# Summing a conditioning vector over 128 partitions: one-column matmuls, or whole-tile transposes and a VectorE row sum

## The chip, the cores and the metric

The kernel runs on one core of a Trainium2 chip. The metric is device time in microseconds (us) of one execution. Before the change the median of three runs is 3439.34 us (3439.0 to 3443.46). All intervals below come from one profiled execution of the kernel before, whose own time stands in the table.

## What is computed

Two transformer blocks with two layers each, on 512 tokens of 1024 features, in fp32; the second block also carries 256 context tokens. Every layer's norms and residuals are steered by six conditioning vectors of 1024 numbers, and it is these vectors that the change touches. Cut to that, the reference is:

```python
cond = jax.nn.silu(c)                                   # 1024 numbers
for layer in range(2):                                  # first block
    mod = (cond @ ada_w[layer] + ada_b[layer])[:, None, :]      # (1024) x (1024 x 6144)
    shift_m, scale_m, gate_m, shift_f, scale_f, gate_f = jnp.split(mod, 6, axis=-1)
    ...
    x = x + gate_f * swiglu(h, ffn_w_in[layer], ffn_w_out[layer])
sc, scc = jax.nn.silu(c), jax.nn.silu(c_ctx)
for l in range(2):                                      # second block
    mx = sc @ w_ada[l] + b_ada[l]                       # for the tokens
    mc = scc @ w_ada[l] + b_ada[l]                      # for the context, same weights
    ...
```

## The kernel before

Feature-major layout: a tensor of 1024 features lies as 8 tiles of 128 partitions by tokens. Every large product is made of three fp32r matmuls (lines 243 to 245): activations and weights are split into a high and a low part (`hh`, `hl`, `gh`, `gl`; `whi`, `wlo`), and high x high, low x high and high x low are added up in PSUM. Weights come by DMA as `raw` tiles of 128x1024 (two buffers), ScalarE casts them to `whi` (line 172) and VectorE makes `wlo` (line 173), three buffers each. One such unit feeds 24 matmuls.

`ffn` (lines 486 to 515, inside `dense`) is the feed-forward stage: for every 128 hidden features TensorE makes a gate and an up product (24 matmuls each), ScalarE takes the silu into `t2a` (line 505), VectorE multiplies (line 507, `t2b`) and the result is split into `gh` and `gl`; after each group of hidden features `out_proj` multiplies by the third weight and VectorE adds into `x` (line 528). Six PSUM banks (`dn`, `d`) rotate through these products, and two more (`tp`) serve small things: the norms' statistics, broadcasts of a column, and the sums that the change is about.

The conditioning vectors are background work. `ada_tasks` (line 288) cuts the product of `cond` and a 1024 x 6144 matrix into groups of 512 output columns, and each group into 8 tasks, one per 128 rows of the matrix. A task loads a 128x512 tile `araw` (line 299) and VectorE multiplies it by a per-partition scalar and adds it into `acc`, 128x512 (lines 308 and 310). After the eighth task `acc` holds 128 partial sums of each of 512 columns, one in every partition, and they must be added over the partitions and turned so that the 512 numbers stand as 128 partitions x 4 columns of `mod`. Four matmuls do that (line 319): each takes 128 columns of `acc` as the stationary operand and a column of ones as the moving one, and writes one column of a `tp` bank. VectorE adds the bias while it copies the four columns out (line 322).

`tick` runs up to three tasks between matmul blocks of a stage, so the group's matmuls stand in TensorE's queue between two blocks of 24. Tile's scheduler sets the order of the instructions on each engine from the program's order and its own estimates. Where `conds` has two vectors, one loaded tile serves two accumulators, and the two groups' sums follow each other.

The vectors of the first block's first layer are made in the opening and in the attention stage. The others are made in three `ffn` stages: those of the first block's second layer (12 groups, one vector), of the second block's first layer (12 groups, two vectors) and of its second layer (4 groups with two vectors, 8 with one). After the first 32 tasks of the middle one `hnorm_now` makes the context's first norm: squares and their column sums (lines 369, 370), a small transpose (375), a power on GpSimd (352), a broadcast by transposes (359).

Of the kernel before, what the change touches and what calls it, by code (L numbers as in the profile page):

```python
# [14 lines left out]
ALU = mybir.AluOpType  # L15
AX = mybir.AxisListType

P = 128
# [121 lines left out]
class Net:  # L140
# [144 lines left out]
        return self.pa.tile([P, 512], F32, tag=tag, bufs=2, name=tag)  # L285


    def ada_tasks(self, w, groups, conds, dsts, bias, bufs=3, bank="st", on_pe=()):

        nc = self.nc
        tasks = []
        for n, g in enumerate([2 * g + i for g in groups for i in range(2)]):
            st = {}
            for k in range(KD):
                def step(g=g, k=k, st=st, pe=n in on_pe):
                    raw = self.accp.tile([P, 512], F32, tag="araw", bufs=bufs, name="araw")
                    nc.sync.dma_start(raw, w[k * P:(k + 1) * P, g * 512:(g + 1) * 512])
                    for i, cond in enumerate(conds):  # L300
                        s = cond[:, k:k + 1]
                        if pe:
                            if k == 0:
                                st[i] = self.psum(bank)
                            nc.tensor.matmul(st[i][:1], lhsT=s, rhs=raw, start=k == 0, stop=k == KD - 1)
                        elif k == 0:
                            st[i] = self.accp.tile([P, 512], F32, tag=f"acc{i}", bufs=1, name="acc")
                            nc.vector.tensor_scalar(st[i], raw, s, None, op0=ALU.mult)
                        else:
                            nc.vector.scalar_tensor_tensor(st[i], raw, s, st[i], op0=ALU.mult, op1=ALU.add)  # L310
                    if k == KD - 1:
                        for i, dst in enumerate(dsts):
                            acc, rows = st[i], 1 if pe else P
                            if pe:
                                acc = self.accp.tile([1, 512], F32, tag="row", bufs=1, name="row")
                                nc.scalar.copy(acc, st[i][:1])
                            ps = self.psum(bank)
                            for j in range(4):
                                nc.tensor.matmul(ps[:, j:j + 1], lhsT=acc[:, j * P:(j + 1) * P], rhs=self.one[:rows],
                                                 start=True, stop=True)  # L320
                            s = slice(g * 4, g * 4 + 4)
                            nc.vector.tensor_add(dst[:, s], ps[:, :4], bias[:, s])
                tasks.append(step)
        return tasks
# [1484 lines left out]
    def block1(self, x):  # L1809
        nc, a, fx = self.nc, self.a, self.fx  # L1810
        cond = self.cond

        def gain(g, i, mod, grp):
            return self.gain(self.v(g, i, 8), mod, grp)

        mod = fx.tile([P, 48], F32, tag="modx", bufs=2, name="mod")
        b = self.v("ada_b", 0, 48)
        with self.pool("rope", side="right") as rp:
            with self.dense():
                for k in range(0, KD, 4):  # L1820
                    nc.sync.dma_start(x[:, k:k + 4], a["xT"][k * P:(k + 4) * P].rearrange("(k p) t -> p k t", p=P))
                self.c_inv = self.load_const(rp, "inv")
                self.c_sgn = self.load_const(rp, "sgn")
                with self.pool("acc", side="right") as self.accp:
                    rope = self.rope_tables(rp, self.accp)
                    self.causal = self.load_const(rp, "causal", BF16)
                    self.lt01 = self.load_const(rp, "lt01")
                    self.ltneg = self.load_const(rp, "ltneg", BF16)
                    self.negtri = self.load_const(rp, "negtri", F32R)
                    self.work["u"] = (self.accp, 8, "t2u", T)  # L1830
                    tasks = self.ada_tasks(a["ada_w"][0], (1, 0), [cond], [mod], b, 12, "dn", (1, 3))
                    A = fx.tile([P, KD], F32, tag="A1", bufs=3, name="A")
                    h, ((stats, apply),) = self.hnorm(x, T, A, mod[:, 0:8], size=T)
                    w = a["attn_w_in"][0][:, 1024:1280]
                    loads = self.load_ahead(*[(w, 0, k, "k") for k in (0, 4)])
                    for i in range(32):
                        tasks[i // 16 * 16 + (1 - i % 2) * 8 + i % 16 // 2]()
                        if i == 7:
                            stats()
                        if i == 15:  # L1840
                            self.gain_scale(A, self.v("norm_mix_g", 0, 8), mod, 1)
                    for load in loads:
                        load()
                    apply()
                self.rope_cs = rope()
            self.bg += self.ada_tasks(a["ada_w"][0], (2, 3, 4, 5), [cond], [mod], b, 2)
            out = []

            def norms(g, i, grp, *loads):
                h, steps = self.hnorm(x, T, gain(g, i, self.mod, grp + 1), self.mod[:, grp * 8:grp * 8 + 8])  # L1850
                out.append(h)
                self.loads = self.load_ahead(*loads)
                return steps

            self.mod = mod
            self.attention(x, h, mod[:, 16:24], a["attn_w_in"][0], a["attn_w_out"][0],
                           lambda: norms("norm_ffn_g", 0, 3, *self.ffn_first(*self.gate_up(a["ffn_w_in"][0]))))
        with self.dense():
            g_in, gate = a["gdn_w_in"][0], mod[:, 40:48]
            mod = self.mod = fx.tile([P, 48], F32, tag="modx", bufs=2, name="mod")  # L1860
            self.bg += self.ada_tasks(a["ada_w"][1], (1, 0, 2, 3, 4, 5), [cond], [mod], self.v("ada_b", 48, 48))
            self.ffn(*self.gate_up(a["ffn_w_in"][0]), a["ffn_w_out"][0], [(out[0], x, T, gate)],
                     lambda: norms("norm_mix_g", 8, 0, (g_in[:, 4096:4112], 0),
                                   *[(g_in[:, c:c + P], 0) for c in (D, 0)]))
        with self.psum_pool(**GDN_BANKS) as self.pp:
            self.gdn(x, out[1], mod[:, 16:24], a["gdn_w_in"][0], a["gdn_w_out"][0],
                     lambda: norms("norm_ffn_g", 8, 3, *self.ffn_first(*self.gate_up(a["ffn_w_in"][1]))))
        return out[2]
# [58 lines left out]
```

## Time and profile before

| | us |
|---|---|
| median of 3 runs (lowest, highest) | 3439.34 (3439.0, 3443.46) |
| the profiled execution | 3443.76 |
| its span, first to last instruction | 3442.0 |
| TensorE (PE) busy, share of the span | 3273.7, 95% |
| VectorE (DVE) busy | 2202.9, 64% |
| ScalarE (ACT) busy | 1274.1, 37% |
| mean granted TensorE clock | 0.981 |

PE is TensorE's matmuls, PEld its weight loads, which overlap them. An instruction's duration in a timeline is longer than the distance to the next one, because matmuls are pipelined: what one costs in a row of matmuls is read from start to start. "Idle before" an instruction is time in which its engine had nothing to run, and the name behind the arrow is what ended it.

### The profile page before, as it was taken

What the parts mean: (1) busy time and instruction counts of PE and PEld (TensorE: products, weight loads), DVE (VectorE), ACT (ScalarE), POOL (GpSimd) and SP (SyncE); (2) the same over time, 40 slices, a digit from 0 to 9 for tenths busy, and PEclk for the clock granted to TensorE, in tenths of its full rate; (3) what the DMA queues carried; (4) which work ended last, traced back from release to release, by engine and by line L of the source; (5) the groups of instructions that cost most, each with busy time, mean ns of one, the idle gap of its engine ahead of it and who ended that gap; (6) DMA issues with size and microseconds to landing.
All of it is one profiled execution on the core that took longest, in us unless ns stands there. A gap on an engine that the chain in (4) does not pass through costs nothing.

```text
span 3442.0 us, 47012 instructions
## 1 busy us (share of the span) xinstructions
PE 3273.7 (95%) x17856; PEld 2692.6 (78%) x17856; DVE 2202.9 (64%) x4517; ACT 1274.1 (37%) x2467; POOL 98.8 (3%) x142
## 2 busy tenths in 40 slices
PE   7998999999999899998999989999999989899999
PEld 4886788878778787887777768888887776778886
DVE  6977655468988676667778777534445875753334
ACT  3566322235443322223644443212123555532222
POOL 4000000000000000000000000000000000000000
PEclk9999999999999999999999999999999999989999
DMA  6655355532112254553343323333332343413332
GB/s 225 171 139 156 120 167 157 161 106 62 44 50 61 65 166 144 155 161 109 115 132 88 113 61 103 107 95 111 117 111 74 114 132 102 126 48 93 98 95 77
DMA packets 480083, 389.79 MB, mean 113 GB/s; under 512 B 21360, under 2 KB 390128, under 8 KB 479856
## 3 DMA queue, kind: packets, MB, share of 16 engines
q1 hardware_dynamic: 479856, 386.77, 38.0%
q8 instruction: 141, 2.31, 0.3%
q14 instruction: 86, 0.70, 0.1%
HBM read 356.28 MB, written 17.83 MB: 109 GB/s over the span
## 4 chain that ended last, share of the span: by engine, by line
PE 43%; DVE 4%; ACT 3%; issue 1%; DMA 1%; POOL 0%; POOLq 0%; DVEq 0%; SPq 0%; ACTq 0%
PE dn L243 6%; PE dn L244 6%; PE dn L245 6%; PE d L243 6%; PE d L244 6%; PE d L245 6%; PE tp L1200 1%; PE s L1236 1%; PE tp L1219 1%; PE tp L1226 1%; ACT pr L1179 1%; DVE cv L1365 1%; DVE wlo L173 1%; PE dn L370 1%; DVE ptl L173 0%
## 5 line engine op out<-in xcount | busy, mean ns | idle before, releaser
L172 ACT CAST whi<-raw 128x1024 fp32r<-128x1024 f32 (+1 forms) x399 | 417.0, 1045 | 785.5 <-PE d L245 433.5
L173 DVE TENSOR_TENSOR wlo<-raw,whi 128x1024 fp32r<-128x1024 f32 (+1 forms) x399 | 486.9, 1221 | 280.0 <-ACT whi L172 279.5
L243 PE MATMUL dn<-hh,whi 128*128 128x512 f32 (+1 forms) x1688 | 619.6, 368 | 8.9 <-ACT t2b L1350 4.5
L245 PE MATMUL dn<-hl,whi 128*128 128x512 f32 (+1 forms) x1688 | 614.1, 365 | 0.0
L244 PE MATMUL dn<-hh,wlo 128*128 128x512 f32 (+1 forms) x1688 | 614.0, 365 | 0.0
L243 PE MATMUL d<-hh,whi 128*128 128x512 f32 (+1 forms) x1120 | 400.7, 358 | 0.0
L244 PE MATMUL d<-hh,wlo 128*128 128x512 f32 (+1 forms) x1120 | 399.9, 357 | 0.0
L245 PE MATMUL d<-hl,whi 128*128 128x512 f32 (+1 forms) x1120 | 399.8, 357 | 0.0
L243 PEld LDWEIGHTS dn<-hh,whi 128*128 128x128 f32 x1688 | 321.5, 191 | 58.0 <-ACT t2b L1350 5.1
L245 PEld LDWEIGHTS dn<-hl,whi 128*128 128x128 f32 x1688 | 321.3, 191 | 46.2 <-issue 2.7
L244 PEld LDWEIGHTS dn<-hh,wlo 128*128 128x128 f32 x1688 | 321.7, 191 | 42.7 <-issue 1.4
L310 DVE SCALAR_TENSOR_TENSOR acc<-araw,cond,acc 128x512 f32<-128x512 f32 x322 | 241.4, 750 | 69.1 <-DMA araw<-in_ada_w 42.2
L243 PE MATMUL d<-gh,whi 128*128 128x512 f32 (+1 forms) x696 | 251.6, 362 | 0.0
L244 PE MATMUL d<-gh,wlo 128*128 128x512 f32 (+1 forms) x696 | 249.9, 360 | 0.0
L245 PE MATMUL d<-gl,whi 128*128 128x512 f32 (+1 forms) x696 | 248.7, 360 | 0.0
L243 PEld LDWEIGHTS d<-hh,whi 128*128 128x128 f32 x1120 | 210.7, 188 | 32.8 <-issue 1.3
L244 PEld LDWEIGHTS d<-hh,wlo 128*128 128x128 f32 x1120 | 210.7, 188 | 32.3 <-issue 1.3
L245 PEld LDWEIGHTS d<-hl,whi 128*128 128x128 f32 x1120 | 210.7, 188 | 31.7 <-DVE hl L390 0.9
L243 PEld LDWEIGHTS d<-gh,whi 128*128 128x128 f32 x696 | 130.6, 188 | 26.2 <-issue 3.1
L245 PEld LDWEIGHTS d<-gl,whi 128*128 128x128 f32 x696 | 130.1, 188 | 24.6 <-issue 2.6
L244 PEld LDWEIGHTS d<-gh,wlo 128*128 128x128 f32 x696 | 130.6, 188 | 23.7 <-issue 2.2
L507 DVE TENSOR_TENSOR t2b<-t2a,d 128x512 f32<-128x512 f32 (+1 forms) x67 | 42.0, 627 | 154.2 <-PE d L245 154.2
(501 smaller groups left out, 5657.9 us busy)
## 6 DMA issues: line engine op xcount, KB each, us to landing
araw<-in_ada_w SPq DMA_DIRECT2D x192, 256.0 KB, 4.0
araw<-in_w_ada SPq DMA_DIRECT2D x192, 256.0 KB, 3.1
raw<-in_ffn_w_in SPq DMA_DIRECT2D x88, 512.0 KB, 4.1
raw<-in_ffn_w_out SPq DMA_DIRECT2D x44, 512.0 KB, 4.5
raw<-in_w_in SPq DMA_DIRECT2D x44, 512.0 KB, 4.0
raw<-in_w_gate SPq DMA_DIRECT2D x44, 512.0 KB, 3.9
raw<-in_w_up SPq DMA_DIRECT2D x44, 512.0 KB, 3.9
raw<-in_w_down SPq DMA_DIRECT2D x44, 512.0 KB, 3.8
```

Of the source, the lines that this page charges most:

```text
L172: nc.scalar.copy(hi, src)
L173: nc.vector.tensor_sub(lo, src, hi.bitcast(F32))
L243: self.nc.tensor.matmul(out, lhsT=lh, rhs=rh, start=j == 0, stop=False)
L244: self.nc.tensor.matmul(out, lhsT=ll, rhs=rh, start=False, stop=False)
L245: self.nc.tensor.matmul(out, lhsT=lh, rhs=rl, start=False, stop=j == n - 1)
L310: nc.vector.scalar_tensor_tensor(st[i], raw, s, st[i], op0=ALU.mult, op1=ALU.add)
L370: nc.tensor.matmul(sums, lhsT=weights(k), rhs=sq, start=k == 0, stop=k == KD - 1)
L507: nc.vector.tensor_mul(y, s, pu[:, :n])
L1179: nc.scalar.activation(pr, s, AF.Exp, bias=st[:, 0:1], accum_out=st[:, 2:3])
L1200: nc.tensor.transpose(tp[:, n * P:(n + 1) * P], pr[:, c:c + P], self.ident)
L1219: nc.tensor.matmul(ps[:64, q0:q1], lhsT=lhs, rhs=pt[sl // 2][0][:, sl % 2, q0:q1].bitcast(F32), start=j == 0, stop=j == nb - 1, skip_group ...
L1226: nc.tensor.matmul(ps[:, q0:q1], lhsT=lhs, rhs=pt[sl // 2][i][:, sl % 2, q0:q1], start=j == 0 and i == 0, stop=j == nb - 1 and i == 1, ski ...
```

## The change

For 52 of the 64 sums, those of the three `ffn` stages, the four one-column matmuls become four 128x128 transposes of `acc` into a whole `tp` bank, 128 partitions x 512. In partition i of the bank now lie the 128 partial sums of column i of each quarter; VectorE adds them along the row, 128x512 to 128x4 (`tensor_reduce`), straight into `mod`, and a second VectorE instruction adds the bias there. The 12 sums of the first layer, in the opening and in the attention stage, keep the matmuls (`turned=False`).

```diff
-    def ada_tasks(self, w, groups, conds, dsts, bias, bufs=3, bank="st", on_pe=()):
+    def ada_tasks(self, w, groups, conds, dsts, bias, bufs=3, bank="st", on_pe=(), turned=True):
...
                             ps = self.psum(bank)
+                            s = slice(g * 4, g * 4 + 4)
+                            if turned:
+                                for j in range(4):
+                                    nc.tensor.transpose(ps[:, j * P:j * P + P], acc[:, j * P:j * P + P], self.ident)
+                                nc.vector.tensor_reduce(dst[:, s], ps.rearrange("p (j q) -> p j q", q=P), axis=AX.X,
+                                                        op=ALU.add)
+                                nc.vector.tensor_add(dst[:, s], dst[:, s], bias[:, s])
+                                continue
                             for j in range(4):
                                 nc.tensor.matmul(ps[:, j:j + 1], lhsT=acc[:, j * P:(j + 1) * P], rhs=self.one[:rows],
                                                  start=True, stop=True)
-                            s = slice(g * 4, g * 4 + 4)
                             nc.vector.tensor_add(dst[:, s], ps[:, :4], bias[:, s])
...
-                    tasks = self.ada_tasks(a["ada_w"][0], (1, 0), [cond], [mod], b, 12, "dn", (1, 3))
+                    tasks = self.ada_tasks(a["ada_w"][0], (1, 0), [cond], [mod], b, 12, "dn", (1, 3), False)
...
-            self.bg += self.ada_tasks(a["ada_w"][0], (2, 3, 4, 5), [cond], [mod], b, 2)
+            self.bg += self.ada_tasks(a["ada_w"][0], (2, 3, 4, 5), [cond], [mod], b, 2, turned=False)
```

The order of the instructions moves a little too. In the listings below the lines of the changed program are 8 higher than before for the same statement behind the edit (507 is 515, 370 is 378, 359 is 367), 310 is 311, and the transposes, the row sum and the addition are lines 322, 323 and 325.

VectorE, around the first sum of the first `ffn` stage that is changed, before:

```order
L507 TENSOR_TENSOR t2b<-t2a,d_4156 128x512
L322 TENSOR_TENSOR mod<-tp,vec 128x4
L308 TENSOR_SCALAR acc<-araw,cond 128x512
L173 TENSOR_TENSOR wlo<-raw,whi 128x1024
L173 TENSOR_TENSOR gl<-t2b,gh 128x512
L310 SCALAR_TENSOR_TENSOR acc<-araw,cond,acc 128x512 x4
```

VectorE at the same place in the changed program:

```order
L515 TENSOR_TENSOR t2b<-t2a,d_4156 128x512
L323 TENSOR_REDUCE mod<-tp 128x4
L309 TENSOR_SCALAR acc<-araw,cond 128x512
L173 TENSOR_TENSOR gl<-t2b,gh 128x512
L325 TENSOR_TENSOR mod<-mod,vec 128x4
L311 SCALAR_TENSOR_TENSOR acc<-araw,cond,acc 128x512
L173 TENSOR_TENSOR wlo<-raw,whi 128x1024
```

The row sum takes the place of the addition, the addition comes three places later, and the weight split `wlo` now stands behind both and behind one more step of the next accumulator. In the stage with two vectors two row sums stand in a row there, and `wlo` keeps its place behind the accumulator's steps.

TensorE, at the fourth pair of sums of the stage with two vectors, where the context's norm follows, before:

```order
L319 MATMUL tp<-one,acc 128x1 x8
L243 MATMUL d_11971<-gh,whi 128x512
L244 MATMUL d_11971<-gh,wlo 128x512
L245 MATMUL d_11971<-gl,whi 128x512
L243 MATMUL d_11971<-gh,whi 128x512
L244 MATMUL d_11971<-gh,wlo 128x512
L370 MATMUL tp<-t2a,mean_d 1x256 x2
```

TensorE at the same place in the changed program:

```order
L322 MATMUL tp<-c_ident,acc 128x128 x8
L243 MATMUL d_11991<-gh,whi 128x512
L244 MATMUL d_11991<-gh,wlo 128x512
L245 MATMUL d_11991<-gl,whi 128x512
L378 MATMUL tp<-t2a,mean_d 1x256 x2
```

The transposes stand where the one-column matmuls stood, and the norm's first column sums come two matmuls sooner. Everywhere else TensorE's queue holds the same blocks, but for a few matmuls that trade places at the end of two stages; ScalarE's and GpSimd's queues are the same, and SyncE's issues the same DMAs.

## Rows read from the trace of the kernel before

**Rows 1.** The page, part 1: busy us, share of the span, instructions of each engine.

```profile
PE 3273.7 (95%) x17856; PEld 2692.6 (78%) x17856; DVE 2202.9 (64%) x4517; ACT 1274.1 (37%) x2467; POOL 98.8 (3%) x142
```

**Rows 2.** Busy by stretch: length, PE, PEld, DVE, ACT, POOL, granted clock, DMA.

```profile
390.00:740.00 350.00, 350.00 (x1616) 290.20 (x1615) 185.23 (x238) 86.00 (x104) 0.00 (x0) 1.00 0.53 163
1200.00:1575.00 375.00, 374.42 (x1801) 310.41 (x1799) 256.70 (x382) 98.52 (x130) 1.07 (x1) 1.00 0.51 154
2130.00:2290.00 160.00, 160.00 (x955) 141.68 (x954) 81.22 (x123) 30.11 (x42) 0.00 (x0) 1.00 0.37 111
2290.00:2635.00 345.00, 345.00 (x2032) 304.95 (x2031) 139.38 (x196) 68.61 (x98) 0.00 (x0) 1.00 0.34 104
```

**Rows 3.** PE's waits, 1205 to 1575: us in total, times, longest. All there are.

```profile
PE tp L359 <- POOL rs_r L352: 0.6, 1, 0.6
```

**Rows 4.** Line 322, 390 to 740, then 1200 to 2635: ns min/median/max, first and last start.

```profile
L322 DVE TENSOR_TENSOR mod<-tp,vec x12: 160/161/163, 410.0 to 738.8; 128x4 f32<-128x4 f32 x12
...
L322 DVE TENSOR_TENSOR modx<-tp,vec x24: 160/162/164, 1229.5 to 2633.1; 128x4 f32<-128x4 f32 x24
L322 DVE TENSOR_TENSOR modc<-tp,vec x16: 161/163/165, 1230.4 to 2277.1; 128x4 f32<-128x4 f32 x16
```

**Rows 5.** PE's timeline, one sum: start us, duration us, engine, line, operation, count.

```profile
408.99 0.95 PE L319 MATMUL tp<-one,acc 128*128 128x1 f32 x8
409.80 0.48 PE L243 MATMUL dn<-hh,whi 128*128 128x512 f32 x1
```

**Rows 6.** PE's timeline, a pair of sums in the stage with two vectors.

```profile
1228.47 1.84 PE L319 MATMUL tp<-one,acc 128*128 128x1 f32 x16
1230.18 0.48 PE L243 MATMUL dn<-hh,whi 128*128 128x512 f32 x1
```

**Rows 7.** PE's timeline, four transposes between two large matmuls (the gated-delta stage).

```profile
1100.52 0.60 PE L1007 MATMUL tp<-c_ident,t2a 128*128 128x128 f32 x4
1100.87 0.47 PE L244 MATMUL dn<-hh,wlo 128*128 128x512 f32 x1
```

**Rows 8.** PE's timeline, six transposes between two large matmuls (a mixer stage).

```profile
1768.67 0.81 PE L1200 MATMUL tp<-c_ident,pr 128*128 128x128 f32 x6
1769.24 0.48 PE L244 MATMUL dn<-hh,wlo 128*128 128x512 f32 x1
```

**Rows 9.** DVE's instructions by line and form, whole span: busy us, mean ns, idle before.

```profile
L1114 DVE TENSOR_REDUCE go_v<-sqo 128x4 f32<-128x512 f32 x8 | 5.5, 684 | 2.5 <-ACT sqo L1111 2.4
L748 DVE TENSOR_REDUCE smx<-sc 128x1 f32<-128x512 f32 x8 | 5.4, 681 | 0.2 <-PE sc L723 0.2
...
L322 DVE TENSOR_TENSOR modx<-tp,vec 128x4 f32<-128x4 f32 x24 | 3.9, 162 | 5.1 <-PE tp L319 4.1
...
L1116 DVE TENSOR_TENSOR go_v<-go_v,rq 128x4 f32<-128x4 f32 x8 | 1.3, 157 | 0.1
```

**Rows 10.** Timelines of DVE and PE, one-vector stage: a weight split and its first use.

```profile
410.45 1.22 DVE L173 TENSOR_TENSOR wlo<-raw,whi 128x1024 fp32r<-128x1024 f32 x1
...
421.01 0.39 PE L244 MATMUL d<-hh,wlo 128*128 128x512 f32 x1
```

**Rows 11.** Timelines of DVE and PE, two-vector stage: a weight split and its first use.

```profile
1235.82 1.22 DVE L173 TENSOR_TENSOR wlo<-raw,whi 128x1024 fp32r<-128x1024 f32 x1
...
1241.39 0.39 PE L244 MATMUL d<-hh,wlo 128*128 128x512 f32 x1
```

**Rows 12.** Timelines of PE and DVE ahead of the context's norm.

```profile
1321.89 1.84 PE L319 MATMUL tp<-one,acc 128*128 128x1 f32 x16
...
1322.09 0.75 DVE L528 SCALAR_TENSOR_TENSOR x<-d,mod,x 128x512 f32<-128x512 f32 x1 [3.29 <-PE d L245]
```

**Rows 13.** As rows 2: transposes among matmuls; after a wait (PE's timeline).

```profile
1099.00:1102.00 3.00, 3.00 (x19) 2.52 (x19) 3.00 (x6) 0.63 (x1) 0.00 (x0) 1.00 0.03 5
...
1632.00:1638.00 6.00, 5.48 (x27) 5.48 (x28) 4.05 (x9) 1.05 (x2) 0.16 (x2) 0.52 0.59 188
...
1632.52 1.11 PE L1442 MATMUL dn<-c_ident,t2b 128*128 128x128 f32 x4 [5.55 <-ACT t2b L1439]
```

## The prediction

> **What bounds the kernel now.** I read the shares of the engines first: TensorE is busy for 95% of the span, VectorE for 64% [rows 1]. A share of the whole says little, so the second view is the busy time by stretch, for the stages that the change touches. In the four stretches that hold them TensorE is busy for 350.00 of 350, 374.42 of 375, 160.00 of 160 and 345.00 of 345 us, at a granted clock of 1.00, the level of 2.4 GHz [rows 2]. Third, who made TensorE wait there: in the stretch with two vectors one wait of 0.6 us, on GpSimd, and nothing on VectorE [rows 3]; in the other stretches no gap is left for one. So in these stages TensorE's own queue is the path. A microsecond that leaves the queue leaves the run, as long as nothing else becomes late. VectorE, which gets the new work, is busy for 185, 257, 81 and 139 us of the same stretches: 53%, 68%, 51% and 40% [rows 2].
>
> **How many sums.** Line 322 runs once per sum: 12 in the first stage, and 24 + 16 in the later ones [rows 4], together the 52 that the change turns. The 16 context sums each follow a sum of the tokens' vector, so the queue has 16 pairs, and 12 + 24 - 16 = 20 single sums.
>
> **What is removed from TensorE.** A single sum is four matmuls, which the trace records as eight pieces. From the first of them to the next large matmul it is 409.80 - 408.99 = 0.81 us; for a pair it is 1230.18 - 1228.47 = 1.71 us [rows 5, 6]. The large matmul behind them has the same duration of 0.48 us behind transposes [rows 5 to 8], so nothing more hangs on the change of kind.
>
> **What is added to TensorE.** The kernel already has fp32 transposes of 128x128, one piece each. Four of them between two large matmuls take 1100.87 - 1100.52 = 0.35 us, six take 1769.24 - 1768.67 = 0.57 us [rows 7, 8], so each further one is (0.57 - 0.35) / 2 = 0.11 us and eight are 0.57 + 0.22 = 0.79 us. The operand is another tile, the shape, type and neighbours are the same. As bounds: if every transpose took the 0.10 us that a piece takes now (0.81 / 8), four would be 0.41 and eight 0.85 us, with the pair's 1.71 / 16 = 0.107 each; if eight cost only twice what four do, they would be 0.70 us. I take 0.35 and 0.79, the rows nearest in kind.
>
> **The sum on TensorE.** 20 x (0.81 - 0.35) = 9.2 us for the singles, 16 x (1.71 - 0.79) = 14.7 us for the pairs: 23.9 us less. With the slow bound it is 20 x 0.40 + 16 x 0.86 = 21.8, with the fast one 9.2 + 16 x 1.01 = 25.4.
>
> **What is added to VectorE.** Each of the 52 sums swaps an addition of 162 ns from PSUM for a row sum of 128x512 to 128x4 and an addition of 128x4 in SBUF. The row sum has its shape in a row of 684 ns, and its source, PSUM, in one of 681 ns; the addition has 157 ns [rows 9]. That is 684 + 157 - 162 = 679 ns more, 52 x 0.679 = 35 us in all. I put it at nothing, because of two covers. The first is the time: the stretches' VectorE work becomes 185 + 8 = 193 of 344.5 us, 257 + 16 = 273 of 364, 81 + 5 = 86 of 156 and 139 + 5 = 144 of 341, so 75% at most. The second is how early VectorE works. What waits behind the row sum and is needed by TensorE soonest is a weight split `wlo`. With three buffers a split is made two blocks ahead: in the stage with one vector it ends at 411.67 and its first reader starts at 421.01, 9.3 us later [rows 10]; with two vectors it ends at 1237.04 for 1241.39, 4.3 us later [rows 11]. There two row sums add 1.36 us, and TensorE comes 0.92 us sooner, 2.3 us together, inside the 4.3. In the first stage the split also lets one accumulator step of 0.7 us pass; 0.68 + 0.7 + 0.46 is far below 9.3. If the cover were gone, each row sum would stand in TensorE's path: that is the second rival.
>
> **What waits on the new instruction.** Row sum and addition wait for the transposes on VectorE's queue as the addition did for the matmuls. The bank is freed by the row sum, so some 0.5 us later; `tp` has two banks and the next sum comes 8 tasks later, so only one place can feel it. Behind the fourth pair the context's norm takes a `tp` bank, and the new order puts its first matmuls two places sooner. The pair starts at 1321.89, so its transposes end near 1322.68, and three large matmuls later, near 1323.4, the norm wants the bank. VectorE is at an update until 1322.84 [rows 12] and then sums for 0.68 us, to 1323.5. That is a wait of some 0.2 us, once. The chain of this norm, with the 0.6 us on GpSimd, is as long as before. The DMAs are the same ones; they follow their buffers and come as much sooner as TensorE does.
>
> **The result of the sum.** 23.9 - 0.2 = 23.7 us. The profiled execution took 3443.76 us, 4.4 above the median of the three, so it would become 3420.1; the median of 3439.34 becomes **3415.6**.
>
> **Rivals.**
> *The gain is taken back where weights are paced by DMA.* In the stage with two vectors VectorE is busiest, and its split frees the `raw` buffer for the next load. If the row sums push that chain past the 4.3 us, TensorE waits for weights and the pairs gain nothing: only 9.2 - 0.2 = 9.0 us are left, 3430.3. For it speaks that DMA, ScalarE and VectorE form a ring there; against it that in 375 us TensorE did not wait for it once [rows 3], and that a pair comes once in some 30 us.
> *VectorE becomes the path, and the kernel is slower.* If each row sum landed whole between TensorE's blocks, a single would cost 0.68 - 0.46 = 0.22 us and a pair 1.36 - 0.92 = 0.44 us: 20 x 0.22 + 16 x 0.44 = 11.4 us more, 3450.7. It decides from the point where a split ends later than its reader, 9.3 and 4.3 us away. The Trainium skill ("VectorE: DVE Perf Modes", Rules for kernel authors) calls this reduction VectorE's slowest operation and advises restructuring where it is on a hot path. By that rule the 35 us count; by the waits here VectorE's queue is not the hot path.
> *The clock falls at the transposes.* After a wait of 5.55 us on TensorE the granted clock of the next 6 us is 0.52, near the lower level of 1.2 GHz; where four transposes stand among matmuls it is 1.00 [rows 13]. If each of the 36 places brought 6 us like that stretch, which lose nearly half, 2.9 us, it would be 104 us more and, less the gain, 3520. The Trainium skill ("TensorE: Matmul & The Clock Gate", Part 4: PE-mode transpose) says that transposes don't count as activity that raises the clock. By that rule the change would be a risk; the stretch with transposes at 1.00 speaks against it here, where they are under 1 us between blocks of matmuls.
> *The change doesn't shorten the queue.* If these transposes ran as two pieces each, as the one-column matmuls do, four would again be eight pieces of 0.1 us: no change, 3439. Rows 7 and 8 show one piece each.
>
> **How the numbers follow.** The forecast gets 0.88, the taken-back gain 0.05, the unshortened queue 0.03, VectorE's path 0.03, the clock 0.01. A measurement of this kernel can tell 0.2% from no change, 6.9 us, so the limit is 3432.5: faster 0.88 + 0.05 = 0.93, same 0.03, slower 0.04. The forecast's own range: the bounds of the transposes give 3414.1 to 3417.7, and the three runs lie over 4.5 us, which also stands for small shifts where stages meet: 3411 to 3422. To hold 8 in 10 it need reach no further; I widen the slow end to 3424 for part of the first rival.
>
> **What would show it.** Right: the stretches between the same blocks are shorter by 5.5, 11.0, 3.7 and 3.7 us (12 singles, 12 pairs, 4 pairs, 8 singles), PE has no idle time there, a single's start to start is 0.35 us and a pair's 0.79, and VectorE's busy time is up by some 35 us. Wrong: waits of L244 on `wlo`, of the norm on the row sum, or a PEclk under 1.00 in these stretches.

## The result, and the profile after

The changed kernel took 3420.76 us in the median (3416.7 to 3421.74, 4 runs), the kernel before 3441.4 us (3439.0 to 3443.69, 4 runs) beside it: 0.9933 of before, interval 0.9919 to 0.9947. It is faster, by 18 to 28 us of 3441. The forecast was 3415.6 us, from a median of before of 3439.34. The profiled execution took 3421.65 us, 22.1 less than the one of before.

The page, part 1, of the changed kernel answers to [rows 1]: TensorE has 26.0 us less, VectorE 25.6 us more, where the forecast had some 35.

```profile
PE 3247.7 (95%) x17648; PEld 2666.4 (78%) x17648; DVE 2228.5 (65%) x4569; ACT 1275.0 (37%) x2467; POOL 100.0 (3%) x142
```

The stretches of [rows 2] in the changed kernel, same columns (length, PE, PEld, DVE, ACT, POOL, granted clock, DMA, GB/s); they are shorter, since the stages are. TensorE still has no room in them and VectorE has: 55%, 73%, 54% and 42%, against the forecast's 56%, 75%, 55% and 42%. The clock stays at 1.00.

```profile
391.00:736.20 345.20, 344.79 (x1568) 284.06 (x1566) 191.02 (x249) 86.54 (x104) 0.00 (x0) 1.00 0.54 165
1197.50:1562.50 365.00, 364.41 (x1710) 299.44 (x1710) 267.20 (x405) 98.75 (x130) 1.08 (x1) 1.00 0.53 159
2118.00:2277.00 159.00, 159.00 (x940) 140.41 (x939) 86.20 (x132) 30.13 (x42) 0.00 (x0) 1.00 0.38 115
2277.00:2617.00 340.00, 340.00 (x1993) 300.25 (x1992) 143.52 (x206) 68.40 (x98) 0.00 (x0) 1.00 0.34 104
```

The timeline of TensorE at the first single sum and the first pair, then VectorE behind the pair (start, duration, engine, line, operation), for [rows 5, 6]. From the transposes to the next large matmul it is 410.42 - 410.07 = 0.35 us and 1226.66 - 1225.87 = 0.79 us. The two row sums of the pair start 0.61 us apart, though each lasts 0.68.

```profile
410.07 0.60 PE L322 MATMUL tp<-c_ident,acc 128*128 128x128 f32 x4
...
410.42 0.47 PE L243 MATMUL dn<-hh,whi 128*128 128x512 f32 x1
410.74 0.39 PE L244 MATMUL dn<-hh,wlo 128*128 128x512 f32 x1
...
1225.87 1.03 PE L322 MATMUL tp<-c_ident,acc 128*128 128x128 f32 x8
...
1226.66 0.47 PE L243 MATMUL dn<-hh,whi 128*128 128x512 f32 x1
1226.97 0.39 PE L244 MATMUL dn<-hh,wlo 128*128 128x512 f32 x1
...
1226.67 0.68 DVE L323 TENSOR_REDUCE modx<-tp 128x4 f32<-128x512 f32 x1
...
1227.28 0.68 DVE L323 TENSOR_REDUCE modc<-tp 128x4 f32<-128x512 f32 x1
```

VectorE's instructions by line and form (busy us, mean ns of one, idle before), for [rows 9]. The row sum has 680 to 687 ns where 684 was expected, the addition 154 where 157 was.

```profile
L323 DVE TENSOR_REDUCE modx<-tp 128x4 f32<-128x512 f32 x24 | 16.5, 687 | 0.1
L323 DVE TENSOR_REDUCE modc<-tp 128x4 f32<-128x512 f32 x16 | 10.9, 680 | 0.0
L323 DVE TENSOR_REDUCE mod<-tp 128x4 f32<-128x512 f32 x12 | 8.2, 682 | 0.0
...
L325 DVE TENSOR_TENSOR modx<-modx,vec 128x4 f32<-128x4 f32 x24 | 3.7, 154 | 0.0
```

TensorE's waits of the changed kernel (total us, times, longest), from 385 to 737, and then from 1200 to 1565, for [rows 3]. The second is the old one on GpSimd. The first is new, but it is in this execution alone: three more of the same kernel (below) have no wait in that stage. There is none from 2115 to 2620.

```profile
PE d L243 <- ACT gh L172: 0.4, 1, 0.4
...
PE tp L367 <- POOL rs_r L360: 0.6, 1, 0.6
```

**By stage.** I cut each trace at the same ScalarE instructions, counted from the start of that engine's queue, so that the pieces hold the same work. "Rest" is the span less the three; its code is the same in all of these kernels but the one that turns the attention stage's sums too. The last two columns are the time against before: the ratio, and its interval.

```
us of the profiled run     one vector  two vectors  last two stages   rest    ratio   95% interval
before                        398.1       415.9          575.9       2052.0
the change                    393.4       405.5          568.6       2052.3   0.9933  0.9919-0.9947
again, e0_change              392.9       405.4          568.6       2051.3   0.9940  0.9927-0.9952
again, e0b_change             393.0       405.4          568.6       2050.1   0.9930  0.9918-0.9943
again, e0c_change             393.2       405.6          568.6       2053.1   0.9937  0.9924-0.9949
e1_transposes_twice           398.2       416.9          575.7       2054.2   1.0009  1.0000-1.0018
e2_rowsum_twice               393.3       408.2          570.4       2048.6   0.9946  0.9932-0.9959
e3_rowsum_six                 393.3       467.3          569.2       2048.2   1.0121  1.0107-1.0135
e4_pairs_only                 398.1       406.3          572.3       2052.5   0.9955  0.9942-0.9967
e5_attention_too              393.1       405.5          570.1       2055.5   0.9943  0.9930-0.9955
e6_no_sums                    392.8       396.3          569.4       2057.9   0.9932  0.9918-0.9945
e7_one_transpose              389.3       397.4          563.5       2052.6   0.9893  0.9875-0.9911
e8_rowsum_no_transpose        391.3       397.0          567.1       2055.6   0.9907  0.9893-0.9921
```

In four profiled executions of the same changed kernel the three stages repeat within 0.5 us, and the rest scatters over 3 us. The stages are the sharper measure, and the ratio is the verdict. One execution of the kernel with one transpose took 5147.81 us at a granted clock of 0.572 and is left out of its ratio.

### The profile page after: what moved, and what is told of

Its sections match the earlier page's. It is cut to its first block, busy times and chain, and to the rows that moved or that the text cites. A ratio compares the mean times of both kernels' runs of the same rounds, so it can differ in the third digit from the quotient of the medians.

```text
span 3419.9 us, 46640 instructions
## 1 busy us (share of the span) xinstructions
PE 3247.7 (95%) x17648; PEld 2666.4 (78%) x17648; DVE 2228.5 (65%) x4569; ACT 1275.0 (37%) x2467; POOL 100.0 (3%) x142
## 4 chain that ended last, share of the span: by engine, by line
PE 43%; DVE 4%; ACT 3%; issue 1%; DMA 1%; POOL 0%; POOLq 0%; DVEq 0%; ACTq 0%
PE dn L243 6%; PE dn L244 6%; PE dn L245 6%; PE d L243 6%; PE d L245 6%; PE d L244 6%; PE s L1244 1%; PE tp L1208 1%; PE tp L1227 1%; PE tp L1234 1%; DVE cv L1373 1%; ACT pr L1187 1%; DVE wlo L173 1%; PE dn L378 1%; DVE st L1184 0%
## 5 line engine op out<-in xcount | busy, mean ns | idle before, releaser
L173 DVE TENSOR_TENSOR wlo<-raw,whi 128x1024 fp32r<-128x1024 f32 (+1 forms) x399 | 486.3, 1220 | 268.5 <-ACT whi L172 267.8
L244 PE MATMUL dn<-hh,wlo 128*128 128x512 f32 (+1 forms) x1688 | 613.3, 364 | 0.0
L244 PE MATMUL d<-hh,wlo 128*128 128x512 f32 (+1 forms) x1120 | 399.9, 357 | 0.0
L244 PEld LDWEIGHTS dn<-hh,wlo 128*128 128x128 f32 x1688 | 321.7, 191 | 42.7 <-issue 1.4
L311 DVE SCALAR_TENSOR_TENSOR acc<-araw,cond,acc 128x512 f32<-128x512 f32 x322 | 241.9, 751 | 68.3 <-DMA araw<-in_ada_w 38.7
L244 PE MATMUL d<-gh,wlo 128*128 128x512 f32 (+1 forms) x696 | 249.8, 359 | 0.0
L244 PEld LDWEIGHTS d<-hh,wlo 128*128 128x128 f32 x1120 | 210.7, 188 | 32.5 <-issue 1.3
L244 PEld LDWEIGHTS d<-gh,wlo 128*128 128x128 f32 x696 | 130.6, 188 | 23.5 <-issue 2.2
```

Of the source, the lines that this page charges most:

```text
L173: nc.vector.tensor_sub(lo, src, hi.bitcast(F32))
L244: self.nc.tensor.matmul(out, lhsT=ll, rhs=rh, start=False, stop=False)
```

## The experiments

Theory T is the prediction's: the time that leaves TensorE's queue leaves the run, and the row sums lie beside it. Its rivals say that the order or something else brought the gain (O), or that VectorE's new work counts (V). The change itself ran three more times as a neighbour of the others.

> The changed kernel as it is, for the comparison with the others on the same chip. Theory T (TensorE's queue is the path in the three stages; the gain is the shorter stay of the 36 places there; VectorE's row sums are free as long as weight splits come in time): 23.7 us less than before, a ratio of 0.993. Every single is 0.35 us and every pair 0.79 us from start to start.

> The changed kernel once more, as the measure for the three that follow. Theory T: 0.993 to 0.994 of before.

> The changed kernel once more, as the neighbour of the two kernels of this group: 0.9935 of the kernel before (0.992 to 0.995 in the runs so far).

Measured: 0.9940, 0.9930 and 0.9937, intervals in the table. The gain repeats.

**All transposes twice.**

```diff
-                                for j in range(4):
+                                for j in [*range(4), *range(4)]:
                                     nc.tensor.transpose(...)
```

> Every one of the 52 sums makes its four transposes twice, into the same bank; the values are the same. Theory T: four transposes more cost 0.79 - 0.35 = 0.44 us at each of the 20 singles and twice that, 0.87 us, at each of the 16 pairs, 22.7 us in all: the kernel is back at the time of before within 3 us (ratio 0.998 to 1.002), VectorE's work unchanged. Rival O (the gain comes from the order that the scheduler made, not from the pieces): the time stays near the changed kernel's, ratio 0.993.

Measured: 1.0009 (1.0000 to 1.0018). The gain is gone, with the row sums still in place. VectorE's order moved a little again, so this run alone doesn't refute O; but TensorE is busy for 345.00 of 345, 363.62 of 365 and 499.00 of 499 us of the stages here, so an order had no idle time to win or lose. TensorE's timeline of this kernel at a single and a pair shows 408.75 - 407.96 = 0.79 us and 1229.77 - 1228.11 = 1.66 us, nearly the 0.81 and 1.71 of [rows 5, 6]: eight transposes cost nearly what four one-column matmuls did.

```profile
407.96 1.03 PE L322 MATMUL tp<-c_ident,acc 128*128 128x128 f32 x8
408.75 0.47 PE L243 MATMUL dn<-hh,whi 128*128 128x512 f32 x1
...
1228.11 1.91 PE L322 MATMUL tp<-c_ident,acc 128*128 128x128 f32 x16
1229.77 0.48 PE L243 MATMUL dn<-hh,whi 128*128 128x512 f32 x1
1230.09 0.40 PE L244 MATMUL dn<-hh,wlo 128*128 128x512 f32 x1
```

**Each row sum twice.**

```diff
-                                nc.vector.tensor_reduce(dst[:, s], ...)
+                                for _ in range(2):
+                                    nc.vector.tensor_reduce(dst[:, s], ...)
```

> Every one of the 52 row sums is made twice, with the same result. Theory T: VectorE's busy time rises by 52 x 0.68 = 35 us and the kernel's time stays, 0.993 of before within 3 us, because the split that TensorE reads next still has some 2 us at the pairs and more at the singles. Rival V (VectorE's work is on the path, and the change would have gained 35 us more without it): 35 us slower than the changed kernel, ratio 1.003.

Measured: 0.9946 (0.9932 to 0.9959). VectorE is busy for 28.6 us more (2258.1 against 2229.5 in the neighbour; 35 were expected), and the ratio moves by 0.0006, inside the intervals. In the table the stage with two vectors is 2.8 us longer, and TensorE has a new wait of 1.6 us there, on `gh` and not on `wlo`: the first sign that the cover there is thin, but far from 28. The last two stages are 1.8 us longer too. That isn't the row sums: the granted clock is 0.83 in the first 10 us there, and the kernel that turns the attention stage too, with the change's code in these stages, has the same 0.83 and 1.5 us.

**Each row sum six times.**

```diff
+                                for _ in range(6):
```

> Every row sum is made six times, with the same result: 3.4 us more per single and 6.8 us per pair on VectorE, 177 us in all. Theory T: the singles stay free (9 us of slack in the one-vector stage), the pairs of the two-vector stage of 512 tokens have some 2 us of slack left, so TensorE waits there for wlo, 4 to 5 us at each of 12 places, 48 to 60 us, and hardly elsewhere: ratio 1.007 to 1.011. Rival V: all 177 us count, ratio 1.045. If VectorE never mattered, 0.993.

Measured: 1.0121 (1.0107 to 1.0135), 62 us over the neighbour, a little beyond the 48 to 60 us that T expected. The place was as T said: the other stages keep their time to 0.6 us, and all of it is in the stage with two vectors. TensorE's waits of this kernel there, 1200 to 1625:

```profile
PE d L244 <- DVE wlo L173: 23.9, 7, 5.4
PE dn L244 <- DVE wlo L173: 12.4, 3, 5.4
PE d L243 <- ACT gh L172: 1.3, 1, 1.3
PE tp L368 <- POOL rs_r L361: 0.4, 1, 0.4
```

The first two rows are waits of L244 on `wlo`, the sign that the prediction named against itself: 36.3 us at 10 places. T had the waits too long, at 48 to 60 us, and left out a second cost that they bring. TensorE's timeline of this kernel at the first of them, then the stretch behind it by busy time and clock:

```profile
1236.78 0.39 PE L243 MATMUL dn<-hh,whi 128*128 128x512 f32 x1
1237.01 0.39 PE L244 MATMUL dn<-hh,wlo 128*128 128x512 f32 x1
...
1242.25 0.80 PE L244 MATMUL d<-hh,wlo 128*128 128x512 f32 x1 [4.18 <-DVE wlo L173]
1242.85 0.63 PE L245 MATMUL d<-hl,whi 128*128 128x512 f32 x1
1243.28 0.63 PE L243 MATMUL d<-hh,whi 128*128 128x512 f32 x1
```

```profile
1243.00:1249.00 6.00, 6.00 (x19) 4.74 (x18) 4.90 (x8) 1.05 (x1) 0.00 (x0) 0.63 0.90 267
...
1197.50:1625.00 427.50, 386.26 (x1740) 313.52 (x1738) 339.46 (x528) 99.44 (x130) 1.56 (x1) 0.95 0.45 135
```

Ahead of the wait the large matmuls start 0.23 us apart, behind it 0.43, and the granted clock of the next 6 us is 0.63. Over the whole stage it is 0.95, where the change has 1.00. At the lower level, 0.5, that is (1.00 - 0.95) / 0.5 x 427.5 = 43 us in which the matmuls take nearly twice their time, some 20 us lost by this estimate. With the waits that makes 56 of the 62 us.

**The pairs alone**, the singles with their old matmuls.

```diff
-                            if turned:
+                            if turned and len(conds) == 2:
```

> Only the 16 pairs of the stages with two vectors are turned (32 of the 52 sums); the 20 singles keep their one-column matmuls. Theory T: the places add up, so 16 x 0.92 = 14.7 us of the 23.9 are left, 9.2 us more than the changed kernel: ratio to before 0.9957. Rival P (the gain in the two-vector stages is partly taken back by late weights, so the singles carry more than their share): under 10 us less than before, above 0.997.

Measured: 0.9955 (0.9942 to 0.9967), 9.3 us over the neighbour's 3420.73, where 9.2 were expected. The one-vector stage is back at 398.1, the time of before.

**The attention stage too.**

```diff
-            self.bg += self.ada_tasks(a["ada_w"][0], (2, 3, 4, 5), [cond], [mod], b, 2, turned=False)
+            self.bg += self.ada_tasks(a["ada_w"][0], (2, 3, 4, 5), [cond], [mod], b, 2)
```

> The 8 sums of the attention stage are turned as well (only the 4 of the opening keep the matmuls). Theory T: TensorE has gaps in that stage and VectorE is busier (three quarters of the stretch), so of 8 x 0.46 = 3.7 us some are lost in waits: 0 to 3.7 us less than the changed kernel, ratio to before 0.9925 to 0.994. Rival V there (the row sum lands on the path of the attention's softmax): 8 x 0.7 = 5 to 6 us more than the changed kernel, 0.9955.

Measured: 0.9943 (0.9930 to 0.9955), 3426.0 against 3420.73. T expected 0 to 3.7 us less; the median is 5.3 us higher, which is what V had there, and the intervals of the two kernels overlap. TensorE's waits in the attention stage, 0 to 380, of this kernel:

```profile
PE tp L378 <- ACT t2a L377: 8.2, 1, 8.2
PE z L798 <- ACT sb_lh L172: 7.0, 6, 4.1
...
PE tp L322 <- DVE acc L311: 3.3, 2, 3.0
```

Here TensorE already waits, for ScalarE and VectorE, and the transposes themselves wait for the accumulator (the last line), so its queue isn't the whole path. The trace shows neither theory's effect. By the same cut, the part up to the one-vector stage, with the opening and the attention in it, took 372.7 us, inside the 371.3 to 375.7 of the four executions of the change, whose scatter is larger than the 3.7 us in question. The 5 us more of this kernel don't stand there, so they are no sign of V; what they are stays open.

**Without the sums.** This kernel leaves the 52 sums over the partitions out; the first four columns of `acc` take their place.

```diff
-                                for j in range(4):
-                                    nc.tensor.transpose(...)
-                                nc.vector.tensor_reduce(...)
-                                nc.vector.tensor_add(dst[:, s], dst[:, s], bias[:, s])
+                                nc.vector.tensor_add(dst[:, s], acc[:, :4], bias[:, s])
```

> The 52 sums over the partitions are left out: no transposes and no row sums, the first four columns of acc take their place (one addition of 128x4 each is left). It tells what the sums still cost after the change. Theory T: 20 x 0.35 + 16 x 0.79 = 19.6 us less than the changed kernel, ratio to before 0.9875, and nothing for the 35 us of row sums. Rival V: 35 us more of VectorE also go, 0.978 or less.

Measured: 0.9932 (0.9918 to 0.9945): no gain over the change, where T expected 20 us. Only the stage with two vectors became shorter, by 9.1 us of the 9.5 expected. In the one-vector stage and the last two, TensorE's waits of this kernel (385 to 800, then 2100 to 2680) show new ones:

```profile
PE d L243 <- ACT gh L172: 3.5, 1, 3.5
...
PE dn L244 <- DVE wlo L173: 2.1, 1, 2.1
PE d L245 <- DVE gl L173: 1.2, 1, 1.2
PE d L244 <- DVE wlo L173: 0.9, 1, 0.9
PE d L243 <- ACT gh L172: 0.9, 1, 0.9
```

Behind the wait of 3.46 us the granted clock is 0.54 for the next 3.5 us, by busy time and clock:

```profile
475.50:479.00 3.50, 3.27 (x7) 2.28 (x8) 2.83 (x5) 1.22 (x2) 0.00 (x0) 0.54 0.87 298
```

VectorE's order had moved by blocks of up to 118 rows: accumulator steps stand bunched in front of the splits and gates that TensorE needs. The timeline of this kernel shows it at the wait of 3.46 us. TensorE waits for `gh`, which is cast from the gate `t2b`; seven accumulator steps stand between the gate before and this one, and the fourth of them had waited 2.57 us for its load. In the change none stands between the same two gates.

```profile
470.17 0.75 DVE L311 SCALAR_TENSOR_TENSOR acc<-araw,cond,acc 128x512 f32<-128x512 f32 x1 [2.57 <-DMA araw<-in_ada_w]
...
474.34 0.68 DVE L511 TENSOR_TENSOR t2b<-t2a,d 128x512 f32<-128x512 f32 x1
...
475.73 0.77 PE L243 MATMUL d<-gh,whi 128*128 128x512 f32 x1 [3.46 <-ACT gh L172]
```

Two theories were left: the order did it (S), or the stages had reached another limit (L). Two more kernels were to tell them apart.

**One transpose instead of four**, all the ties kept; three of the four transposes of each sum are left out, so the row sum reads a quarter as much.

```diff
-                                for j in range(4):
-                                    nc.tensor.transpose(ps[:, j * P:j * P + P], acc[:, j * P:j * P + P], self.ident)
-                                nc.vector.tensor_reduce(dst[:, s], ps.rearrange("p (j q) -> p j q", q=P), axis=AX.X,
+                                nc.tensor.transpose(ps[:, :P], acc[:, :P], self.ident)
+                                nc.vector.tensor_reduce(dst[:, s], ps[:, :P].rearrange("p (j q) -> p j q", q=32), axis=AX.X,
```

> Leaves out three of the four transposes of each sum; the row sum then adds 128 columns to four sums of 32, so the sums are not the reference's. The instructions that tie VectorE to TensorE stay, and so does nearly all of the order on every queue. It is to settle why leaving out the sums altogether gained nothing. By rows of the change, each transpose is 0.11 us, so a single loses 0.33 and a pair 0.66 us: 20 x 0.33 + 16 x 0.66 = 17 us on TensorE. Theory S (the order did it: without a TensorE instruction in the chain VectorE's accumulator steps are bunched, and TensorE then waits): here the order is kept, so the 17 us come out, 0.9885 of the kernel before (0.9865 to 0.9905), with the stages shorter than in the change by 4.0 us (12 singles), 7.9 us (12 pairs) and 5.3 us (4 pairs and 8 singles). Rival L (the stages have reached another limit, such as the ring of weight loads, splits and buffers, and a shorter queue no longer shortens them): about 0.993, with waits of L244 on wlo or of L243 on gh where the change has none.

Measured: 0.9893 (0.9875 to 0.9911). The stages are shorter than in the neighbour by 3.9, 8.2 and 5.1 us, where S expected 4.0, 7.9 and 5.3. L falls: the same queue, kept in its order, gives back what is taken from it. A pair with its two transposes now takes 1221.82 - 1221.68 = 0.14 us, in TensorE's timeline of this kernel:

```profile
1221.68 0.38 PE L321 MATMUL tp<-c_ident,acc 128*128 128x128 f32 x2
1221.82 0.48 PE L243 MATMUL dn<-hh,whi 128*128 128x512 f32 x1
1222.13 0.39 PE L244 MATMUL dn<-hh,wlo 128*128 128x512 f32 x1
```

**Row sums without transposes.** The transposes are left out, and the row sum reads `acc` itself.

```diff
-                                for j in range(4):
-                                    nc.tensor.transpose(...)
-                                nc.vector.tensor_reduce(dst[:, s], ps.rearrange("p (j q) -> p j q", q=P), axis=AX.X,
+                                nc.vector.tensor_reduce(dst[:, s], acc.rearrange("p (j q) -> p j q", q=P), axis=AX.X,
```

> Leaves out the transposes alone: the row sum reads the accumulator itself, along its own rows, so the sums are not the reference's, but VectorE keeps all its work (52 row sums of 128x512, now from SBUF). Again no TensorE instruction stands in the chain, and the order on VectorE and SyncE moves by blocks, as it did without the sums. Theory S: the same outcome as without the sums, 0.993 of the kernel before (0.990 to 0.997), with new waits of L243 on gh or L244 on wlo of 3 to 15 us in all. Rival V (what the kernel without the sums lost had nothing to do with the order; a shorter TensorE queue by itself brings the gain as soon as VectorE has its pace back): 0.9875, 20 x 0.35 + 16 x 0.79 = 20 us under the change.

Measured: 0.9907 (0.9893 to 0.9921), 11 us under the neighbour where V wanted 20. It lies inside the range of S, but the interval holds neither S's 0.993 nor V's 0.9875: part of the gain came. The stages gain 1.9, 8.6 and 1.5 us of the 4.2, 9.5 and 6.0 that the removed transposes are worth by 0.35 and 0.79 (5.3, 10.4 and 7.0 by the fuller price at the end of this text). TensorE's new waits on `gh`, `gl` and `wlo` come to 7.1 us in the three stages, of the 3 to 15 that S expected; 1.8 of them are on `gh` in the one-vector stage. With more work on VectorE than without the sums, it is no slower. So what the two kernels lack is the tie to TensorE, not VectorE's time. That the bunched order makes the waits is shown at the one place above and argued for the others; a kernel with that order forced back, and no transposes, wasn't tried. Why the rest of the kernel without the sums is 5 to 8 us longer than the change's, in the same code, stays open too: its stages gained 8.5 us over the neighbour's, and the rest took nearly all of it back.

None of the kernels that compute what the reference does is faster than the change.

## Why the prediction was right

**The queue's price.** The forecast took 0.81 to 0.35 us for a single and 1.71 to 0.79 for a pair; the timeline has 0.35 and 0.79. Matching the large matmuls of both traces place by place, each single moved the run by 0.45 to 0.46 us and each pair by 0.90 to 0.92: 5.5 + 11.0 + 3.6 + 3.6 = 23.7 us, where the forecast had 23.9. By the cut at ScalarE's instructions the stages lost 4.7 + 10.4 + 7.3 = 22.4 us, with the ends of the stages and the new wait in it; the three other executions, without that wait, lost 22.7 to 23.0. That the transposes carry it is shown by doubling them (no gain left) and by leaving three of four out (17.2 us more), not only by the sum. The price from the sum to the next large matmul is not the whole price, as the last section shows; what it leaves out is the same before and after, so the difference holds.

**The cover.** "I put it at nothing" held: twice the row sums cost 2 to 3 us in the stage with two vectors and nothing that the ratio can tell. One sign of being right came out smaller: VectorE's busy time rose by 25.6 us, not 35. The durations did add up to 35, by line 35.6 + 8.1 us for the row sums and additions less some 8.4 for the old additions; but VectorE's instructions overlap (the second row sum starts 0.61 us behind a first of 0.68), so busy time grew by less than their sum. The reason given held as well. In the changed kernel a split of that stage ends near 1235.8 (two in a row from 1234.61 take 2.35 us, the first half of it) and its reader starts at 1237.90, 2.1 us later, where the forecast left 4.3 - 2.3 = 2.0 us:

```profile
1234.61 2.35 DVE L173 TENSOR_TENSOR wlo<-raw,whi 128x1024 fp32r<-128x1024 f32 x2
...
1237.90 0.39 PE L244 MATMUL d<-hh,wlo 128*128 128x512 f32 x1
```

Six row sums instead of one use it up, in that stage alone.

**The small terms.** The wait of the norm on the row sum was put at 0.2 us; the trace has L378 wait for L323 once, 0.4 us on the weight load, and the matmuls lost nothing by it: from the last large matmul to the norm's first it is 1318.24 - 1317.92 = 0.32 us, and 1324.94 - 1324.61 = 0.33 before. So that term was too large by 0.2. One wait was not foreseen: at 691.90 TensorE waits 0.41 us for `gh`, behind an accumulator step that had waited for its `araw` load. It isn't the change's: the three other executions don't have it.

**The rivals.** The taken-back gain wanted waits on `wlo` in the stage with two vectors; the trace has none, and the pairs alone bring their part, 9.3 us short of the whole. The unshortened queue is out: four transposes are four pieces in the trace. VectorE as the path is refuted at one and two row sums and real at six. The clock stayed at 1.00 in all four stretches; the transposes didn't lower it, also where twice as many stand together. They stand there for under 2 us between large matmuls, so the runs don't tell what a long row of them would do. The Trainium skill ("VectorE: DVE Perf Modes", Rules for kernel authors), which the forecast weighed, calls the reduction VectorE's slowest operation. Here it isn't: the row sum of 128x512 takes 0.68 us, the split `gl` of that size 0.69 and an accumulator step 0.75 (the lines of L173 and L311 by form). Nor is it on a hot path here.

**The 5 us between 3415.6 and 3420.76.** 2.1 of them are the start: the kernel before had a median of 3441.4 beside the change, not 3439.34. The other 3.1 are the difference of 23.7 and 20.6 us between the medians. The four comparisons give ratios of 0.9930 to 0.9940, or 20.7 to 24.1 us, and the code that is the same scatters by 3 us from one profiled execution to the next, so no cause is to be sought there.

## What to carry to other kernels

Where TensorE has no gap in a stage, an operation that isn't part of its main stream is priced from start to start in the timeline, and moving part of it to an engine with time is worth just the difference, as long as what the other engine makes next is ready a little earlier than it is read; that distance, 9.3 and 4.3 us here, is to be read first. Fewer instructions aren't always less time: leaving out the step that makes VectorE follow TensorE let a scheduler bunch VectorE's work, and the waits that followed, with the lower clock behind them, took back about half of what the shorter queue should have given. A stage in which TensorE already waits for others, as in attention here, showed no gain from the same edit.

## What the runs showed that was not expected

A wait on TensorE can cost more than its length. Behind waits of 3.46 and 4.18 us in stages that otherwise run at 1.00, the granted clock was 0.54 and 0.63 in the next 3.5 and 6 us, and large matmuls started 0.43 instead of 0.23 us apart; six row sums lost 36 us to waits and some 20 to the clock.

What a transpose costs doesn't all stand in front of the next large matmul. One, two, four, eight and sixteen in a row take 0.03, 0.14, 0.35, 0.79 and 1.66 us from their start to the next large matmul, as if the first were nearly free. But that matmul's successor then comes 0.31 or 0.32 us behind it, where large matmuls otherwise start 0.23 apart. From the transposes to the second large matmul it is 0.34, 0.45, 0.67, 1.10 and 1.98 us; less the 0.23 that a large matmul takes anyway, that is 0.11, 0.22, 0.44, 0.87 and 1.75: 0.11 us for every transpose, the first included. The four one-column matmuls of [rows 5] have the same 0.09 behind them (their second large matmul starts at 410.12), so they cost 0.90 and not 0.81 us. TensorE's timeline of the kernel with one transpose:

```profile
409.81 0.27 PE L321 MATMUL tp<-c_ident,acc 128*128 128x128 f32 x1
409.83 0.48 PE L243 MATMUL dn<-hh,whi 128*128 128x512 f32 x1
410.15 0.40 PE L244 MATMUL dn<-hh,wlo 128*128 128x512 f32 x1
```
